# One layer of a hybrid encoder: two input products as one Winograd pair, weights of q and k kept split, the residual kept in the result's rows

## The chip, the core and the metric

The kernel runs on one core of a Trainium2 chip. The metric is the device time of one execution in microseconds; the median of several runs counts. TensorE (PE) multiplies, VectorE (DVE) and ScalarE (ACT) work on whole tiles of 128 partitions, GpSimd (POOL) computes powers and issues some DMAs, SyncE (SP) issues the other DMAs.

## The reference

One layer, 2048 rows of 1024 values, all in float32. The parts that matter here:

```
y = rmsnorm(h, pre_mix_g)                    # h = x, 2048 x 1024
z = y @ w_in                                 # 1024 x 2576
zu, zv, zq, zk, zvb, zg, zlr = split(z)      # 512, 512, 256, 256, 512, 512, 16 columns
a = gmlp_mixer(zu, zv, ...)                  # per 128 rows: layernorm(gelu(zv)), a product along the rows, times gelu(zu)
b = gla_mixer(zq, zk, zvb, zg, zlr, ...)     # gated linear attention, state carried over chunks of 64 rows, times silu(zg)
h = h + rmsnorm(concat(a, b) @ w_out, post_mix_g)
f = square(relu(rmsnorm(h, pre_ff_g) @ w_ff1)) @ w_ff2
out = h + rmsnorm(f, post_ff_g)
```

## The kernel before

**Products.** A float32 operand is held as two halves: hi, a copy rounded to the multiplier's format, and lo, the rest. `mm3` (L146 to L148) is one product of two such pairs and issues three matmuls: hi by lo, hi by hi, lo by hi. ScalarE makes hi with a cast, VectorE makes lo with a subtraction (`split_lo`, L143). `load_w` loads 128 rows of a weight into a tile of the ring `ws`, casts and splits it.

**First phase.** The 2048 rows go in four blocks b of 512 rows, each of four tiles of 128. `group` computes one set of columns of z for a block, in eight k-steps of four tiles by three matmuls; g, vb, v and u are 512 columns wide, q 272 (with zlr), k 256. Block 0 runs g, vb, q, k, v, u; the other blocks run vb, q, k, g, then `out_proj` of the block before (o, 16 steps), v, u. The four sums of each product lie in four PSUM banks and are evicted by `keep`: zq and zk by VectorE (L592), the rest by ScalarE with `lookup` (L301).

**Jobs.** After certain k-steps, `jobs.tick` runs pieces of the other work of a block, and so puts their matmuls between the groups' own: `gla` (decay products `cm` and `dc`, transposes `qk` of qe and ke, scores `sc`, updates `up`, the products `o`, transposes of zg), `spatial` (`mixd`), `gate` (zu times zv at L441, the sum of squares at L443, a power on POOL at L156, the scaling at L445, then transposes `pt` of zu by `put`, L286) and `hpost` (the rows of h after the mixer). A job is queued when its group is done and is stepped by the ticks that follow, so the gates of block b - 1 and the last chunks of its attention fall into the first steps of block b.

**Order.** In the first phase the order on TensorE is that of the code; on the other engines a scheduler orders the instructions. From the first FFN product on, the order of all engines is that of the code.

**FFN.** Both products are done in seven block products for eight (the table `WINO`: for p1 to p7 the left part, the right part and the bank chain A, B or C; s1 to s4 and t1 to t4 are sums of blocks). The first (banks `pf_`) keeps its result in `f_d`; the second (banks `po_`) runs in two passes over 1024 rows each, with eight chunks a pass, reads right-hand tiles `tt` from `t_d` and adds its banks into tiles `acc`.

**Result.** `hpost` stores the rows after the mixer to `h_d`. At the end of a pass `evac` puts for each half row of 128x512 a sum of squares, a root, a `scale` (L1092) and a `give` into a list, from which `some` takes units as the slots go by; `read_h` brings the rows of `h_d` back on POOL's queue, `give` adds them on VectorE (L512) and stores the sum to `out`, from POOL in pass 0 and from SP in pass 1.

## Time and profile before

| what | value |
|---|---|
| median of 3 runs | 2029.22 us (2028.96 to 2031.94) |
| the profiled execution | 2030.61 us, its span 2028.8 us |
| TensorE busy | 1991.7 us, 98% of the span |
| VectorE, ScalarE, POOL busy | 68%, 47%, 13% |
| mean granted clock of TensorE | 0.996 |
| DMA | 467.83 MB, 231 GB/s on average |
| last matmul | starts 13.65 us after 2000 us of the span |

The profile is one execution, recorded by the hardware. A busy time is the sum of an engine's instructions; a row of waits tells what an engine stood idle for before an instruction; the granted clock is the share of full speed that TensorE was given. The start of one instruction to the start of the next on TensorE is the pitch, since matmuls overlap.

### The profile page before, as it was taken

The numbers are of one execution on the slowest core, as the hardware profiler recorded it, in microseconds if no ns is written. First come the engines' busy times: TensorE is split into PE (matmuls) and PEld (weight loads), VectorE is DVE, ScalarE is ACT, GpSimd is POOL, SyncE is SP. The second block draws the span as 40 slices with busy tenths as digits, with TensorE's granted clock in tenths as the row PEclk, the third lists the DMA queues.
The fourth block names the chain that finished last, engine by engine and source line by source line (L and its number), as shares of the span: only waits on it lengthen the run. The fifth ranks groups of instructions, "written<-read, shape, count | busy, mean of one in ns | idle before, by whom it ended". The sixth has DMA issues, their size and how long they took to land.

```text
span 2028.8 us, 27534 instructions
## 1 busy us (share of the span) xinstructions
PE 1991.7 (98%) x9504; PEld 1650.7 (81%) x9504; DVE 1388.8 (68%) x2443; ACT 948.1 (47%) x1894; POOL 268.1 (13%) x442
## 2 busy tenths in 40 slices
PE   8999999999999999999999999999999999999996
PEld 7989888988888887888887888888888888788885
DVE  4484467236735756657678777665888888989877
ACT  5463465236433446566667766665212215222212
POOL 0020311002100200013331333320000002100011
PEclk9999999999999999999999999999999999999998
DMA  7434744535783586758888888888676778876674
GB/s 225 133 113 132 236 154 146 177 132 159 219 279 112 169 289 201 261 188 279 283 278 301 295 285 287 267 279 300 237 269 238 246 262 295 296 265 241 244 277 176
DMA packets 174683, 467.83 MB, mean 231 GB/s; under 512 B 24768, under 2 KB 49872, under 8 KB 160848
## 3 DMA queue, kind: packets, MB, share of 16 engines
q1 hardware_dynamic: 145376, 368.01, 53.7%
q0 software_dynamic: 29168, 98.06, 13.6%
q8 instruction: 75, 1.23, 0.2%
q14 instruction: 64, 0.52, 0.1%
HBM read 331.77 MB, written 134.22 MB: 230 GB/s over the span
## 4 chain that ended last, share of the span: by engine, by line
PE 55%; DVE 2%; DMA 2%; issue 1%; ACT 1%; POOL 0%; DVEq 0%; POOLq 0%; ACTq 0%; SPq 0%
PE pf_A L146 6%; PE pf_A L148 6%; PE pf_A L147 6%; PE po_A L147 5%; PE po_A L146 5%; PE po_A L148 5%; PE pf_C L146 3%; PE pf_C L148 3%; PE pf_C L147 3%; PE po_C L147 2%; PE po_C L146 2%; PE po_C L148 2%; PE pf_B L148 1%; PE pf_B L147 1%; PE pf_B L146 1%; PE po_B L147 1%
## 5 line engine op out<-in xcount | busy, mean ns | idle before, releaser
L512 DVE TENSOR_TENSOR acc<-acc,po_A 128x512 f32<-128x512 f32 x232 | 159.2, 687 | 47.9 <-PE po_A L148 33.6
L962 ACT CAST sh_s<-r 128x512 fp32r<-128x512 f32 x96 | 55.6, 618 | 170.2 <-PE po_A L148 93.5
L962 ACT CAST sh_a<-f 128x512 fp32r<-128x512 f32 x94 | 54.6, 618 | 127.9 <-DMA f<-f_d 94.9
L143 DVE TENSOR_TENSOR wl_s<-s,wh_s 128x512 fp32r<-128x512 f32 x96 | 66.2, 689 | 60.7 <-ACT wh_s L725 60.6
L146 PE MATMUL pf_A<-hl_t,wh_s 128*128 128x512 f32 x256 | 102.1, 399 | 5.1 <-ACT uy L907 2.5
L146 PE MATMUL pp_o<-wl_o,abh 128*128 128x512 f32 x256 | 102.9, 402 | 0.3 <-DVE h L469 0.2
L146 PE MATMUL po_A<-tt,sh_s 128*128 128x512 f32 x256 | 100.5, 393 | 2.7 <-DVE acc L512 2.6
L148 PE MATMUL pf_A<-hh_t,wl_s 128*128 128x512 f32 x256 | 101.6, 397 | 0.0
L146 PE MATMUL po_C<-tt,sh_s 128*128 128x512 f32 x256 | 100.4, 392 | 0.7 <-DMA tt<-t_d_b 0.7
L147 PE MATMUL pf_A<-hh_t,wh_s 128*128 128x512 f32 x256 | 100.9, 394 | 0.0
L147 PE MATMUL po_A<-tt,sh_s 128*128 128x512 f32 x256 | 100.8, 394 | 0.0
L147 PE MATMUL po_C<-tt,sh_s 128*128 128x512 f32 x256 | 100.8, 394 | 0.0
L148 PE MATMUL pp_o<-wh_o,abl 128*128 128x512 f32 x256 | 99.9, 390 | 0.0
L147 PE MATMUL pp_o<-wh_o,abh 128*128 128x512 f32 x256 | 99.7, 390 | 0.0
L148 PE MATMUL po_C<-tt,sl_s 128*128 128x512 f32 x256 | 99.5, 389 | 0.0
L148 PE MATMUL po_A<-tt,sl_s 128*128 128x512 f32 x256 | 99.5, 389 | 0.0
L146 PE MATMUL po_A<-tt,sh_a 128*128 128x512 f32 x248 | 97.6, 393 | 1.3 <-DMA tt<-t_d_t 1.1
L147 PE MATMUL po_A<-tt,sh_a 128*128 128x512 f32 x248 | 97.6, 394 | 0.0
L512 DVE TENSOR_TENSOR acc<-acc,po_C 128x512 f32<-128x512 f32 x120 | 82.4, 687 | 21.3 <-PE po_C L148 13.8
L148 PE MATMUL po_A<-tt,sl_a 128*128 128x512 f32 x248 | 96.4, 389 | 0.0
L143 DVE TENSOR_TENSOR wl_a<-w1s,wh_a 128x512 fp32r<-128x512 f32 x96 | 65.9, 688 | 42.4 <-ACT wh_a L725 42.2
L512 DVE TENSOR_TENSOR uy<-uy,pf_C 128x512 f32<-128x512 f32 x62 | 42.4, 684 | 42.1 <-ACT uy L909 40.4
(301 smaller groups left out, 5917.5 us busy)
## 6 DMA issues: line engine op xcount, KB each, us to landing
tt<-t_d_t SPq DMA_DIRECT2D x61, 1024.0 KB, 6.0
tt<-t_d_b SPq DMA_DIRECT2D x46, 1024.0 KB, 4.8
w1s<-in_w SPq DMA_DIRECT2D x64, 512.0 KB, 4.8
f<-f_d SPq DMA_DIRECT2D x64, 512.0 KB, 7.0
w2s<-in_w POOLq DMA_DIRECT2D x32, 512.0 KB, 6.5
t_d_t<-th_t POOLq DMA_DIRECT2D x64, 256.0 KB, 5.0
t_d_t<-tl_t POOLq DMA_DIRECT2D x64, 256.0 KB, 4.9
f_d<-ux SPq DMA_DIRECT2D x30, 512.0 KB, 5.8
```

Source lines behind the costliest of these rows:

```text
L143: v.tensor_tensor(out_lo, src, hi.bitcast(F32), ALU.subtract)
L146: pe.matmul(ps, ahi, blo, start=start, stop=False, **kw)
L147: pe.matmul(ps, ahi, bhi, start=False, stop=False, **kw)
L148: pe.matmul(ps, alo, bhi, start=False, stop=stop, **kw)
L512: eng.tensor_tensor(out_, x_, y_, ALU.add)
L962: a.copy(hi, src)
```

## The change

- `pair` computes vb and g of blocks 1 to 3 together, after k, as one product of a 512x1024 left side with a 1024x1024 right side in seven products of blocks: p1, p2, p5, p6, p7, p4, p3. Each takes four k-steps with two tiles of 128 rows. A chain (A, B or C) has two banks; p1, p6, p7 and p4 use chain A in turn, and its banks are copied out by ScalarE in between.
- `sums_w`, ticked in block 0, loads the rows of w_in for both groups, makes the four right-hand sums t1 to t4 and stores them to `v_d`.
- `load_s`, in every second k-step of group k, loads the rows of xt for two k again, scales them, makes the four left-hand sums and splits them.
- `load_q` stores the split weights of q and k to `q_d` in block 0 (32 stores from POOL) and loads the halves from there in the other blocks.
- The rows after the mixer are stored straight into `out`. `give` adds the scaled halves there by an accumulating DMA from POOL, except for rows 15, 10 and 11, which come back by SP and are added and stored as before.
- The sums of y for the FFN in block 3 (`sums(0, k)`) are queued after the pair and not before vb.

The core of the diff:

```diff
+    h_d = [out[i * P:(i + 1) * P, :] for i in range(NT)]
...
+    def load_q(b, g, k):
+        n = q_d[g, k].shape[-1]
+        if b == 0:
+            hi, lo = load_w(f"{b}_{g}", w_in, GROUPS[g], k)
+            pool.dma_start(q_d[g, k][:, 0, :], hi.bitcast(F32))
+            pool.dma_start(q_d[g, k][:, 1, :], lo.bitcast(F32))
+            return hi, lo
...
+        loads[f"{b}_{g}"] = dma.dma_start(hi.bitcast(F32), q_d[g, k][:, 0, :]).ins
+        dma.dma_start(lo.bitcast(F32), q_d[g, k][:, 1, :])
+        return hi, lo
...
+    def sums_w(k):
...
+            st = wp.tile([P, D], F32, name=f"vs{k}_{c}", tag="xr", bufs=4)
+            dma.dma_start(st, w_in[(k + 4 * c) * P:(k + 4 * c + 1) * P, 1536:2560])
...
+        minus(v, t1, b12, b11)
+        minus(v, t2, b22, t1)
+        minus(v, b12, b22, b12)
+        minus(v, b21, b21, t2)
+        for n, t in enumerate((t1, t2, b12, b21)):
+            dma.dma_start(v_d[k][:, n, :], t)
...
+    def load_s(b, k):
+        y1, y2 = stage(f"xs1_{b}_{k}"), stage(f"xs2_{b}_{k}")
+        for t, kk in ((y1, k), (y2, k + 4)):
+            dma.dma_start(t, xt[kk * P:(kk + 1) * P, b * TB:(b + 1) * TB])
+            a.activation(t, t, AF.Copy, scale=gpre[:, kk:kk + 1])
...
+        plus(v, a22, a21, a22)
+        minus(v, a21, a11, a21)
+        minus(v, a11, a22, a11)
+        minus(v, a12, a12, a11)
+        for n, t in enumerate((y1, y2)):
+            a.copy(hi[:, n * 512:(n + 1) * 512], t)
+            split_lo(lo[:, n * 512:(n + 1) * 512], t, hi[:, n * 512:(n + 1) * 512])
...
+    def pair(b, ss_):
...
+        for m, n in enumerate(PAIR):
...
+            for k in range(4):
+                if right[0] == "t":
+                    st = stage(f"ws_{b}_{n}_{k}")
+                    loads[f"{b}_pair"] = dma.dma_start(st, v_d[k][:, int(right[1]) - 1, :]).ins
...
+                    a.copy(wh, st)
+                    split_lo(wl, st, wh)
...
+                for t in range(2):
...
+                    mm3(chains[chain][t], *lh, wh, wl, k == 0 and not begun, k == 3, skip_group_check=True)
...
+                elif n == "p6":
+                    zg_[t] = slot(f"zg_{i0 + t}", tag="four")
+                    a.copy(zg_[t], A[t])
...
-            if b == NB - 1:
-                jobs.add(*((lambda k=k: sums(0, k), 1) for k in range(4)))
-            group(b, "vb", AF.Copy)
...
+            jobs.add(*((lambda k=k: sums_w(k), 1) for k in range(4)))
...
+        def before_k(k):
+            if b > 0 and k % 2:
+                ss_.append(load_s(b, k // 2))
...
-        group(b, "k", None)
+        group(b, "k", None, before_k)
         if b > 0:
-            group(b, "g", AF.Silu, lambda k: finish(b - 1, 1) if k == KT - 1 else None)
+            pair(b, ss_)
+        if b == NB - 1:
+            jobs.add(*((lambda k=k: sums(0, k), 1) for k in range(4)))
...
+    def give(i, hf):
+        cs = slice(hf * 512, (hf + 1) * 512)
+        if i in res:
+            plus(v, res[i][hf], res[i][hf], halves[i, hf])
+            dma.dma_start(out[i * P:(i + 1) * P, cs], res[i][hf])
+        else:
+            pool.dma_start(h_d[i][:, cs], halves[i, hf], accum_op=ALU.add)
...
+                    if final and slot_ % 28 == 4:
+                        for row_ in (2 * NPAIR - 1, NPAIR - 2, NPAIR - 1):
+                            read_h(p * 2 * NPAIR + row_)
```

TensorE at the start of block 2, before: behind the third k-step of vb stand the transposes `pt4_0` and `pt5_0` of the gated rows of tiles 4 and 5 of block 1. The number that ends a name tells tiles apart.

```order
L146 MATMUL pp_2_vb_3_3814<-wl_2_vb_2_3876,yh_2_2_3583 128x512
L147 MATMUL pp_2_vb_3_3814<-wh_2_vb_2_3875,yh_2_2_3583 128x512
L148 MATMUL pp_2_vb_3_3814<-wh_2_vb_2_3875,yl_2_2_3584 128x512
L286 MATMUL pt4_0_3891<-ident_213,zu_4_3779 128x128 x4
L286 MATMUL pt5_0_3900<-ident_213,zu_5_3781 128x128 x4
L146 MATMUL pp_2_vb_0_3811<-wl_2_vb_3_3912,yh_2_3_3626 128x512
L147 MATMUL pp_2_vb_0_3811<-wh_2_vb_3_3911,yh_2_3_3626 128x512
```

The same place after; `put` is at L402 and `mm3` at L151 to L153 there.

```order
L151 MATMUL pp_2_q_3_3984<-wl_q2_2_4042,yh_2_2_3755 128x272
L152 MATMUL pp_2_q_3_3984<-wh_q2_2_4041,yh_2_2_3755 128x272
L153 MATMUL pp_2_q_3_3984<-wh_q2_2_4041,yl_2_2_3756 128x272
L402 MATMUL pt4_0_4057<-ident_217,zu_4_3951 128x128 x4
L402 MATMUL pt5_0_4066<-ident_217,zu_5_3953 128x128 x4
L151 MATMUL pp_2_q_0_3981<-wl_q2_3_4076,yh_2_3_3798 128x272
L152 MATMUL pp_2_q_0_3981<-wh_q2_3_4075,yh_2_3_3798 128x272
```

The transposes still stand behind the third step of the block, which is now one of q, 272 columns wide. The decay products of chunks 2 and 3 in block 1 have moved from vb to q in the same way.

VectorE at that place, after: `xs1` and `xs2` are the left-hand sums of `load_s`, L557 and L561 are the gate's two steps (L441 and L445 before).

```order
L628 TENSOR_TENSOR xs2_2_0_4202<-xs1_2_0_4201,xs2_2_0_4202 128x256
L631 TENSOR_TENSOR xs1_2_0_4201<-xs1_2_0_4201 128x256
L557 TENSOR_TENSOR zu_4_3951<-zu_4_3951,zv_4_3600 128x512
L557 TENSOR_TENSOR zu_5_3953<-zu_5_3953,zv_5_3602 128x512
L631 TENSOR_TENSOR xs1_2_0_4201<-xs2_2_0_4202,xs1_2_0_4201 128x256
L160 TENSOR_SCALAR rs_a4_4000<-ssa4_3998 128x1
L631 TENSOR_TENSOR xs2_2_0_4202<-xs2_2_0_4202,xs1_2_0_4201 128x256
L549 TENSOR_TENSOR zv_6_3604<-mixd6_3965,bs_225 128x512
L561 TENSOR_SCALAR zu_4_3951<-zu_4_3951,rs_a4_4000 128x512
```

Sums of `load_s` now stand among the steps of the gate, where splits of vb's weights stood.

VectorE at the end of the kernel, before: `hr` is a residual's half row, L1092 the scale.

```order
L1092 SCALAR_TENSOR_TENSOR acc1_22_3_16598<-acc1_22_3_16598,rs_f15_18920,pfg_13916 128x512
L512 TENSOR_TENSOR hr15_1_18677<-hr15_1_18677,acc1_22_3_16598 128x512
L1092 SCALAR_TENSOR_TENSOR acc1_21_3_16701<-acc1_21_3_16701,rs_f15_18920,pfg_13916 128x512
L512 TENSOR_TENSOR hr15_0_18676<-hr15_0_18676,acc1_21_3_16701 128x512
L1092 SCALAR_TENSOR_TENSOR acc1_12_2_16542<-acc1_12_2_16542,rs_f10_18958,pfg_13916 128x512
```

After, from the last add of a product (`po15_B_3`) on:

```order
L628 TENSOR_TENSOR acc1_11_3_16843<-acc1_11_3_16843,po15_B_3_19225 128x512
L1202 TENSOR_TENSOR ssf10_19193<-ssf10_19193 128x1
L160 TENSOR_SCALAR rs_f10_19236<-ssf10_19193 128x1
L628 TENSOR_TENSOR hr15_18970<-hr15_18970,acc1_22_3_16928 128x512
L1202 TENSOR_TENSOR ssf11_19208<-ssf11_19208 128x1
L160 TENSOR_SCALAR rs_f11_19242<-ssf11_19208 128x1
L1208 SCALAR_TENSOR_TENSOR acc1_21_3_17015<-acc1_21_3_17015,rs_f15_19197,pfg_14248 128x512
L628 TENSOR_TENSOR hr15_18970<-hr15_18970,acc1_21_3_17015 128x512
```

Behind that add stood one residual's add and seven pairs of a scale and an add; one add and five pairs stand there now, since row 14's halves need no add on VectorE. All other rows of the result but 10 and 11 have lost that add too.

## Rows read from the trace of the kernel before

**Rows 1.** The page, busy time of each engine, share of the span, instructions.

```profile
PE 1991.7 (98%) x9504; PEld 1650.7 (81%) x9504; DVE 1388.8 (68%) x2443; ACT 948.1 (47%) x1894; POOL 268.1 (13%) x442
```

**Rows 2.** Waits of TensorE: who waits for whom, us in total, times, longest.

```profile
PE po_A L146 <- DVE acc L512: 2.6, 1, 2.6
PE pf_A L146 <- ACT uy L907: 2.5, 1, 2.5
PE pf_A L146 <- ACT u L907: 2.2, 1, 2.2
PE po_A L146 <- DMA tt<-t_d_t: 1.1, 1, 1.1
PE po_C L146 <- DMA tt<-t_d_b: 0.7, 1, 0.7
PE pf_A L146 <- ACT u L903: 0.4, 1, 0.4
```

**Rows 3.** Windows behind three waits: stretch, its length, busy by engine, PEclk, DMA share, GB/s.

```profile
779.44:782.86 3.42, 3.42 (x9) 2.53 (x9) 2.56 (x5) 3.10 (x6) 0.00 (x0) 0.50 0.49 153
1093.47:1096.88 3.41, 3.41 (x9) 2.65 (x8) 3.41 (x6) 3.41 (x8) 0.00 (x0) 0.50 0.40 162
1748.00:1752.00 4.00, 4.00 (x19) 3.30 (x18) 4.00 (x8) 0.00 (x0) 0.00 (x0) 1.00 1.00 312
```

**Rows 4.** Timeline of TensorE: start, duration, line, operation. FFN, then q's first, k's first.

```profile
1979.82 0.39 PE L146 MATMUL po_C<-tt,sh_s 128*128 128x512 f32 x1
1982.57 0.39 PE L146 MATMUL po_A<-tt,sh_s 128*128 128x512 f32 x1
...
52.29 0.28 PE L146 MATMUL pp_q<-wl_q,yh 128*128 128x272 f32 x1
64.32 0.28 PE L146 MATMUL pp_k<-wl_k,yh 128*128 128x256 f32 x1
```

**Rows 5.** Timeline of VectorE at the end of pass 1.

```profile
1991.49 0.74 DVE L1092 SCALAR_TENSOR_TENSOR acc<-acc,rs_f,pfg 128x512 f32<-128x512 f32 x1
...
2014.09 0.69 DVE L512 TENSOR_TENSOR acc<-acc,po_B 128x512 f32<-128x512 f32 x1
...
2015.89 0.74 DVE L1092 SCALAR_TENSOR_TENSOR acc<-acc,rs_f,pfg 128x512 f32<-128x512 f32 x1
...
2024.99 0.69 DVE L512 TENSOR_TENSOR hr<-hr,acc 128x512 f32<-128x512 f32 x1
```

**Rows 6.** DMA issues: count, KB each, median us from issue to landing.

```profile
out<-hr POOLq DMA_DIRECT2D x16, 256.0 KB, 8.2
```

**Rows 7.** Timeline of ScalarE in the first group: first and seventh cast of ws_g.

```profile
6.63 0.62 ACT L217 CAST wh_g<-ws_g 128x512 fp32r<-128x512 f32 x1 [0.45 <-DMA ws_g<-in_w_in]
...
19.10 0.62 ACT L217 CAST wh_g<-ws_g 128x512 fp32r<-128x512 f32 x1 [0.33 <-DMA ws_g<-in_w_in]
```

**Rows 8.** Groups by line, shapes apart: count, busy us, mean ns, idle before, releaser.

```profile
L143 DVE TENSOR_TENSOR wl_vb<-ws_vb,wh_vb 128x512 fp32r<-128x512 f32 x32 | 21.7, 688 | 16.2 <-ACT wh_vb L217 12.3 <-DMA trif<-in_sel 3.5
L592 DVE TENSOR_SCALAR zq<-pp_q,rx 128x272 f32<-128x272 f32 x16 | 6.9, 494 | 3.1 <-PE pp_q L148 3.1
L907 ACT COPY uy<-pf_A 128x512 f32<-128x512 f32 x31 | 18.1, 585 | 17.0 <-PE pf_A L148 15.5 <-DMA f_d<-ux 0.7 <-DMA f_d<-uy 0.7
```

**Rows 9.** Timelines of TensorE and VectorE, start of block 2; in brackets the idle before.

```profile
337.79 0.50 PE L146 MATMUL pp_vb<-wl_vb,yh 128*128 128x512 f32 x1 [0.75 <-ACT zu L301]
...
343.78 0.49 DVE L445 TENSOR_SCALAR zu<-zu,rs_a 128x512 f32<-128x512 f32 x1 [0.43 <-POOL rs_a L156]
...
346.41 1.03 PE L286 MATMUL pt<-ident,zu 128*128 128x128 f32 x8
...
347.55 0.49 DVE L445 TENSOR_SCALAR zu<-zu,rs_a 128x512 f32<-128x512 f32 x1 [0.44 <-POOL rs_a L156]
```

**Rows 10.** Timelines of VectorE and TensorE in vb of block 1.

```profile
143.43 0.42 DVE L143 TENSOR_TENSOR lal<-xs,lah 128x256 fp32r<-128x256 f32 x1
...
143.94 0.28 PE L333 MATMUL cm<-lal,trir 128*128 128x256 f32 x1
```

94 lines of the change are left out of this document (66 added, 28 removed).

## Prediction

> **What bounds the kernel now.** I read the page first. TensorE is busy for 1991.7 us, 98% of the span, VectorE for 68% [rows 1], so the time is its matmuls, its few waits, a start and a tail; no other engine comes near. Next I read its waits after the start; those that the argument needs are in [rows 2]: three of 2.2 to 2.6, which are the longest, and some of about 1 or less. Third, the granted clock: after two of these three waits TensorE ran 3.4 us at 0.50, its lower level of 1.2 GHz, and after the third it stayed at 1.00 [rows 3], so a wait of some 2 us may cost 1.7 us more. Fourth, the pitch of the matmuls: twelve of 128x512 start within 2.75 us, 0.229 each, and the 96 of a q group within 12.03 us, 0.125 each, so a k-step of twelve takes 2.75 us in a wide group and 1.50 in q [rows 4]. Everything beside this must be hidden behind these steps, and where a step is short, less is hidden.
>
> **What goes.** For each of blocks 1 to 3, vb and g were 2 x 8 x 12 = 192 matmuls and are 7 x 4 x 2 x 3 = 168. That is 3 x 24 = 72 fewer, at 0.229 **-16.5 us**, all on the bound engine. The Trainium skill ("TensorE: Matmul & The Clock Gate", Part 1) gives N/2.4 GHz + 2.5 ns, about 216 ns, for a back-to-back matmul; the pitch here is longer, and by the page's figure this term would be -15.5.
>
> At the end, rows of the result are accumulated by DMA in place of read, added and stored. VectorE ends 11.0 us after its last add of a product, which ended at 2014.09 + 0.60: one add of a residual, seven pairs of a scale and an add, 1.39 us a pair by their starts, and small ones [rows 5]. After, one add and five pairs stand there: 0.6 + 5 x 1.39 + 0.4 of small ones, 8.0. **-3.0** (-2 to -3.5: a root of the last two rows may come late). The reads of h go from 4 MB to 1.5 MB, so the last loads of tt should not wait: -1.1 and -0.7 [rows 2], **-1.8** (0 to -1.8, since SP now issues the three reads left ahead of two of those loads). In the middle, where pass 0 ends, VectorE loses sixteen adds of a residual and their waits for buffers, and the wait of 2.6 on acc [rows 2] should go: **-2.6**, or 0 if accumulating transfers hold the acc buffers for long. No row shows such a transfer; the nearest is out<-hr of the same size on the same queue, 8.2 us from issue to landing [rows 6], and I take that, at which the buffers come free some us before they are wanted. The Trainium skill ("DMA: Bandwidth & Descriptors", Anatomy of one DMA) fits 2.0 us + bytes/436e3 to a transfer issued from GpSimd, which makes 2.6 us of 256 KB as an estimate; no run here shows it, and the sum stays as it is by either. Together **-23.9**.
>
> **What comes, and what is moved.** The pair takes a right-hand tile of 256 KB for every six matmuls, 1.37 us, where a group took one per 2.75. In the first group ScalarE's casts of ws_g run from 6.63 to 19.10, seven of them, so six intervals, with a tile of xt in each: twelve tiles in 12.5 us, 1.04 each. A tile costs ScalarE a cast of 0.62 [rows 7] and VectorE a split of 0.69 [rows 8], both below 1.37, and no job is ticked into long waits there. So the pair itself costs nothing. The cost is in the cover that vb's and g's long steps gave to other chains:
>
> - **Gates of blocks 2 and 3.** The transposes of the gated rows stood after the third k-step of vb, 8.6 us into it. They now stand after the third of q, 4.5 us in, and the second two after the fourth. The chain's ends by the trace, counted from vb's start at 337.79: zu_5 at 343.78 + 0.49, 6.5 us; zu_7 at 347.55 + 0.49, 10.25 us [rows 9]. If it takes as long now, TensorE waits 6.5 - 4.5 = 2.0, spends 0.8 on transposes and 1.5 on a step, and waits 10.25 - 8.8 = 1.45: 3.4 a block, **+6.9**. In the chain two casts and three splits for vb and q go (q's weights arrive split), while the first two k of load_s bring four scalings and two casts to ScalarE and some eight subtractions of 128x256 and two splits to VectorE. That may move its end by 1.5 either way or, where a DMA of load_s is late, more: 0.5 to 6 a block.
> - **Block 1.** There the decay products cm stood behind the third k-step of vb, at 143.94, so vb began three steps, some 8.3, before; the operand of the second pair was written at 143.43 + 0.42, at +8.2, with nothing to spare [rows 10]. In q the first pair is wanted at +4.5 and the second 0.8 later: 8.2 - 5.3 = 2.9. The later steps (transposes of qe and ke, scores, the o products, transposes of zg) stand on q's and k's short steps too; by the same reckoning only the last comes late, by 0.6, and the yl and the sums of load_s ahead on VectorE may add 0.5. **+4.0** (1.5 to 6).
> - **The clock.** Each of these three places has a wait of 2 to 3 us. By [rows 3] two in three such waits lost 1.7 us; short matmuls around them may make it more or less likely. I take one and a half: **+2.5** (0 to 5.1).
> - **Block 0.** sums_w puts two loads of 512 KB and four subtractions per k into vb, q and k. A split of k's weights then stands behind four evictions of zq, 0.49 each, and three subtractions of 0.69 [rows 8]: 4.0 us, of which two steps hide most: **+1.5** (0 to 3). The loads stand on SP's queue ahead of some of xt and ws_g in the first group: **+0.4** (0 to 1). The stores of q's and k's halves are 32 issues on POOL's queue, which has nothing urgent there: nothing.
> - **Start of the pair.** VectorE evicts four zk, 2.0 us, behind or before the first splits: up to 1.3 a block, I take 0.3: **+1.0** (0 to 3.9).
> - **Banks.** p6, p7 and p4 share two banks. Between the last matmul of one tile and the next product's first stand three matmuls, 0.69 us, and ScalarE needs 0.585 for the copy of a bank [rows 8], after the matmul's end and perhaps behind a cast. The nearest row is a wait of 0.4 on such a copy [rows 2]. 0.2 at each of six places: **+1.2** (0 to 3).
> - **Block 3.** The four sums of FFN inputs are ticked later, into o, v and u, whose steps are long: **+0.3** (0 to 1).
>
> In all **+17.8**, so -6.1 net. The profiled execution took 2030.61 us, 1.8 more than its span, and would take 2024.5; the median of three runs was 2029.22, and from there it is **2023.1**, -0.3%.
>
> **The rivals.**
> A, the cover holds. For: 64 casts and splits of q's and k's weights are gone in blocks 1 to 3 from the two engines that feed the chains, and each of the chains has idle time in it, 0.43 and 0.44 us on VectorE before two of its scalings of zu [rows 9], which wait for POOL alone. Against: the positions in TensorE's order are earlier by 4 us and the chain needs some 6 to 10. Then about 4 of the 17.8 are left and the time is 2009.
> B, the losses eat the gain. Gates at 5 a block, block 1 at 5, three windows at half clock, the pair's start at 1 each: 10 + 5 + 5.1 + 3 + 1.5 = 24.6 against 23.9, so 2029 to 2030: no change.
> C, the pair isn't bound by TensorE, so the change does not do what it says: if tiles come at 1.60 us and not below 1.37, 84 of them cost 19 us, with the rest at its middle 2042. Against it stand [rows 7], at 1.04.
> D, slower by the accumulating transfers. They are 26, on one queue with eight in flight; if they run one after the other at the 8.2 us of [rows 6], the last pass has ten from the first scale at 1991.49 [rows 5] (some 16 earlier now), and the end moves from 2024 to about 2057. It decides from some 5.7 us each; below that the ten are done before the six stores that are left. For it: an accumulate reads what it writes. Against: reads of h of twice the size, four of them issued together, landed side by side.
>
> **How the numbers follow.** The forecast has 0.50, A 0.15, B 0.22, C 0.05, D 0.08. About 0.2% (4 us) is what a measurement of this kernel can tell from no change. The forecast's terms spread by some 7 us to either side (2016 to 2030), most from the gates. It gives 0.43 to faster and 0.07 to the same; A is faster; B is the same, with 0.04 of it slower; C and D are slower. So faster 0.58, the same 0.25, slower 0.17. The range runs from near A's time to past B's: 2011 to 2032, which leaves out D, C and the cheapest ends.
>
> **What would show it.** TensorE's instructions down by 72, its busy time by about 16 us. Waits of TensorE on zu or on the transposes' operand in the fourth k-step of q in blocks 2 and 3, 1 to 3 us each; one on lal in block 1; dips of the granted clock behind them. Inside the pair no waits but short ones on banks, a product of 24 matmuls in 5.5 us. No wait on acc near 1730, none on tt near the end, and five pairs of scale and add after TensorE's last matmul, 12 us or so to the end of the span in place of 15. It is wrong if a product of the pair takes over 6 us, if the accumulating transfers land after 10 us or in a row, or if q's steps show no wait at all (then A).

## The result: 1.5% slower, and where the time went

The changed kernel takes **2060.72 us** (median of 4 runs, 2058.15 to 2063.51) and the kernel before, beside it, 2029.09 (4 runs, 2027.84 to 2031.94): a ratio of **1.0153, interval 1.0141 to 1.0165**. That is slower by some 31 us where 6 less were forecast. The profiled execution has a span of 2061.4 us, 32.6 more than before.

The page of the profile after, its rows of busy time and of the granted clock (columns as in [rows 1]):

```profile
PE 1997.4 (97%) x9432; PEld 1649.2 (80%) x9432; DVE 1434.1 (70%) x2511; ACT 984.1 (48%) x1942; POOL 286.1 (14%) x464
...
PEclk9999999999999999999999999999999999999999
```

The 72 matmuls are gone, 9504 to 9432, yet TensorE is busy for 5.7 us more than in [rows 1], where 16 less were expected, and idle for 26.9 more (2061.4 - 1997.4 against 2028.8 - 1991.7). The first says that the same matmuls went slower somewhere, which is the clock or a spacing too small to be a wait; the second asks for the waits. The row of the clock can't tell, since a short stretch at half speed leaves a slice at 9.

Waits of TensorE after (columns as in [rows 2]), the longest groups:

```profile
PE pp_q L151 <- ACT zu L417: 8.9, 5, 3.1
PE pp_g L151 <- ACT yh L207: 6.9, 1, 6.9
PE pp_q L151 <- DVE wl_q L148: 5.6, 2, 4.2
PE pt L402 <- DVE zg L527: 4.4, 4, 2.3
PE po_C L151 <- DMA tt<-t_d_t: 3.3, 1, 3.3
PE pp_k L151 <- DVE wl_k L148: 3.1, 1, 3.1
PE pf_A L151 <- ACT uy L1028: 2.5, 1, 2.5
...
PE pp_o L151 <- DVE h L585: 2.1, 1, 2.1
PE pp_v L151 <- DVE zk L708: 1.9, 1, 1.9
...
PE pt L402 <- DVE zu L561: 1.2, 2, 0.7
```

Before, all waits came to 21.6 us, after to 51.4. The start (pp_g) was there, and the waits on uy and u as in [rows 2]. New are the first matmul of q on ScalarE's eviction of zu, 8.9 (before, vb's first waited 1.7 there, in two blocks together); q and k on their own weights, 8.7; transposes on zg; po_C on a load of tt; pp_o on h. The wait that the prediction was about, transposes on zu in q, is the last row: 1.2 in all.

Windows behind four of these waits (columns as in [rows 3]):

```profile
363.60:367.00 3.40, 3.24 (x13) 2.98 (x14) 3.38 (x9) 3.40 (x8) 0.71 (x1) 0.50 0.47 165
69.98:73.40 3.42, 3.42 (x18) 3.42 (x17) 2.27 (x6) 0.00 (x0) 2.51 (x5) 0.51 1.02 265
773.20:776.60 3.40, 3.40 (x10) 2.62 (x9) 3.05 (x5) 2.29 (x5) 0.00 (x0) 0.50 1.06 392
1746.00:1749.40 3.40, 3.40 (x10) 2.66 (x9) 0.00 (x0) 0.58 (x1) 0.86 (x1) 0.50 1.07 351
```

There are nine such stretches of 3.4 us at the lower level, 1.2 GHz, each behind a wait of 2.1 us or more, where before had the two of [rows 3]. Seven more by 1.7 us each are 12 us, more than half of what TensorE's busy time is above its forecast.

By stages, from the first matmul of each group in the timeline of TensorE (us, before and after, worked out from those starts):

| stage | before | after | difference |
|---|---|---|---|
| start, g and vb of block 0 | 52.3 | 52.9 | +0.7 |
| q and k of block 0 | 23.5 | 38.2 | **+14.7** |
| v and u of block 0 | 59.8 | 62.4 | +2.6 |
| block 1: vb, q, k, g; after: q, k, pair | 80.5 | 85.4 | **+4.8** |
| block 2, the same | 69.3 | 69.1 | -0.3 |
| block 3, the same | 69.4 | 69.0 | -0.4 |
| o, v, u of blocks 1, 2 and 3 | 361.4 | 369.1 | **+7.6** |
| the last o | 46.8 | 50.9 | **+4.1** |
| FFN, both products | 1250.4 | 1251.5 | +1.1 |
| last matmul to the end | 15.2 | 12.9 | **-2.3** |

They add up to 32.6. A wait ahead of q's first matmul stands in the row of the u before it, so 2.4 of each u's excess belongs to the next block's q.

The pair itself does what it should. In block 2 it runs from 393.46 to 432.81 without a wait:

```profile
393.46:432.81 39.35, 39.35 (x170) 31.29 (x169) 20.23 (x32) 21.42 (x34) 0.00 (x0) 1.00 0.64 202
```

168 matmuls in 39.35 us are 0.234 each, against the 0.229 of [rows 4], with the clock at 1.00, and VectorE and ScalarE are busy for little more than half of it. The groups that it replaces were shorter than [rows 4] say: g of blocks 2 and 3 took 21.8 us before, 0.227 a matmul. So a pair saves 2 x 21.8 - 39.4 = 4.2 us and not 24 x 0.229 = 5.5, some 12.6 in three blocks. The Trainium skill ("TensorE: Matmul & The Clock Gate", Part 1) gives about 216 ns for a back-to-back matmul of this width; all three pitches here are longer.

**First place: the start of q in blocks 1 to 3.** ScalarE and then TensorE at the start of block 2; L302 is the scaling in `load_s`, L417 the eviction of zu from PSUM:

```profile
356.37 0.72 ACT L302 ACTIVATE xs<-xs,gpre 128x512 f32<-128x512 f32 x1 [4.84 <-DMA xs<-in_xt]
362.41 0.72 ACT L302 ACTIVATE xs<-xs,gpre 128x512 f32<-128x512 f32 x1 [5.32 <-DMA xs<-in_xt]
363.04 1.82 ACT L417 ACTIVATE zu<-pp_u,rx 128x512 f32<-128x512 f32 x3
```

```profile
363.76 0.59 PE L151 MATMUL pp_q<-wl_q,yh 128*128 128x272 f32 x1 [2.60 <-ACT zu L417]
```

The scheduler put two scalings of `load_s` ahead of the evictions of zu. The second waits 5.32 us for its transfer, and behind it stand evictions that could have run: they free the PSUM banks that q needs. The last matmul of u starts at 358.98, before the wait for that transfer is over. TensorE waits 2.60 (2.40 and 3.09 in the other two blocks), and the clock is at half from 363.6.

**Second place: q and k of block 0.** SP's queue, then VectorE (L285 and L295 are the loads and stores of `sums_w`, L215 a load of weights, L631 its subtractions), then TensorE:

```profile
54.53 2.40 SPq L295 DMA_DIRECT2D v_d<-vt  x2
...
59.84 0.92 SPq L285 DMA_DIRECT2D vs<-in_w_in  x2
60.87 0.89 SPq L215 DMA_DIRECT2D ws_q<-in_w_in  x2
...
65.23 2.49 SPq L295 DMA_DIRECT2D v_d<-vt  x2
```

```profile
64.51 0.69 DVE L631 TENSOR_TENSOR vt<-vs 128x512 f32<-128x512 f32 x1 [2.86 <-DMA vs<-in_w_in]
66.67 0.69 DVE L631 TENSOR_TENSOR vt<-vs,vt 128x512 f32<-128x512 f32 x1 [1.47 <-DMA vs<-in_w_in]
...
69.00 0.44 DVE L148 TENSOR_TENSOR wl_q<-ws_q,wh_q 128x272 fp32r<-128x272 f32 x1 [0.44 <-ACT wh_q L222]
```

```profile
69.50 0.39 PE L151 MATMUL pp_q<-wl_q,yh 128*128 128x272 f32 x1 [4.22 <-DVE wl_q L148]
...
78.71 0.39 PE L151 MATMUL pp_k<-wl_k,yh 128*128 128x256 f32 x1 [3.06 <-DVE wl_k L148]
```

VectorE waits for vs with the splits of q's weights behind it; SP's stores wait for VectorE (8.2 us for vt from 52 to 92) with the loads of those weights behind them. A split of k's weights waits 5.1 us besides, for the store of an earlier half out of its buffer. The DMA engines are full there:

```profile
53.00:72.00 19.00, 13.44 (x98) 13.00 (x97) 9.03 (x17) 2.91 (x8) 6.22 (x13) 0.95 1.01 342
```

**Third place: the last o.** VectorE splits hl_b and hl_t for the FFN there, the sums that the change ticks later, and one waits 1.33 us for a cast, which itself waits 1.40 for its transfer; the eviction of pp_o stands behind, and TensorE waits 2.1 for it:

```profile
768.69 2.00 DVE L148 TENSOR_TENSOR hl_b<-hl_b,hh_b 128x512 fp32r<-128x512 f32 x3 [1.33 <-ACT hh_b L673]
770.67 0.69 DVE L148 TENSOR_TENSOR hl_t<-hl_t,hh_t 128x512 fp32r<-128x512 f32 x1
771.28 1.88 DVE L585 TENSOR_TENSOR h<-pp_o,pg 128x512 f32<-128x512 f32 x3
```

All three have one form: an instruction that waits for a transfer, itself or through a cast, stands on an in-order engine ahead of one that could run, and TensorE waits for the latter. The third is read from the trace alone: no run moves it, and the last o took 47.3 to 51.4 us in the other kernels that have the pair, which all tick these sums at the same place. The theory after this reading: the loss is the order in which the sums' instructions stand, not the bytes they move and not the products. Its rivals: the transfers themselves (DMA bandwidth), the stores of q's and k's halves, and the residual part.

### The profile page after: what moved, and what is told of

It reads as the page before. It is cut to its first block, busy times and chain, and to the rows that moved or that the text cites. A ratio compares the mean times of both kernels' runs of the same rounds, so it can differ in the third digit from the quotient of the medians.

```text
span 2061.4 us, 27763 instructions
## 1 busy us (share of the span) xinstructions
PE 1997.4 (97%) x9432; PEld 1649.2 (80%) x9432; DVE 1434.1 (70%) x2511; ACT 984.1 (48%) x1942; POOL 286.1 (14%) x464
## 4 chain that ended last, share of the span: by engine, by line
PE 58%; DVE 1%; ACT 1%; DMA 1%; issue 0%; DVEq 0%; ACTq 0%
PE po_A L152 6%; PE po_A L151 6%; PE pf_A L151 6%; PE po_A L153 6%; PE pf_A L153 5%; PE pf_A L152 5%; PE po_C L151 3%; PE po_C L152 3%; PE po_C L153 3%; PE pf_C L151 3%; PE pf_C L153 3%; PE pf_C L152 3%; PE po_B L152 1%; PE po_B L151 1%; PE po_B L153 1%; PE pf_B L151 1%
## 5 line engine op out<-in xcount | busy, mean ns | idle before, releaser
L628 DVE TENSOR_TENSOR acc<-acc,po_A 128x512 f32<-128x512 f32 x232 | 159.6, 688 | 60.6 <-PE po_A L153 32.1
L148 DVE TENSOR_TENSOR wl_s<-s,wh_s 128x512 fp32r<-128x512 f32 x96 | 66.2, 689 | 61.8 <-ACT wh_s L846 61.7
L151 PE MATMUL pf_A<-hl_t,wh_s 128*128 128x512 f32 x256 | 101.6, 397 | 5.1 <-ACT uy L1028 2.5
L151 PE MATMUL pp_o<-wl_o,abh 128*128 128x512 f32 x256 | 104.0, 406 | 2.2 <-DVE h L585 2.1
L151 PE MATMUL po_C<-tt,sh_s 128*128 128x512 f32 x256 | 101.7, 397 | 3.3 <-DMA tt<-t_d_t 3.3
L151 PE MATMUL po_A<-tt,sh_s 128*128 128x512 f32 x256 | 101.0, 394 | 0.0
L153 PE MATMUL po_C<-tt,sl_s 128*128 128x512 f32 x256 | 100.9, 394 | 0.0
L153 PE MATMUL pf_A<-hh_t,wl_s 128*128 128x512 f32 x256 | 100.9, 394 | 0.0
L153 PE MATMUL pp_o<-wh_o,abl 128*128 128x512 f32 x256 | 100.7, 393 | 0.0
L153 PE MATMUL po_A<-tt,sl_s 128*128 128x512 f32 x256 | 100.4, 392 | 0.0
L628 DVE TENSOR_TENSOR acc<-acc,po_C 128x512 f32<-128x512 f32 x120 | 82.5, 688 | 25.0 <-PE po_C L153 16.1
L151 PE MATMUL po_A<-tt,sh_a 128*128 128x512 f32 x248 | 97.8, 394 | 0.0
L153 PE MATMUL po_A<-tt,sl_a 128*128 128x512 f32 x248 | 97.3, 392 | 0.0
L161 POOL TENSOR_TENSOR rs_f<-rs_f,mhalf 128x1 f32<-128x1 f32 x16 | 13.5, 846 | 578.7 <-DVE rs_f L160 578.7
```

Source lines behind the costliest of these rows:

```text
L148: v.tensor_tensor(out_lo, src, hi.bitcast(F32), ALU.subtract)
L151: pe.matmul(ps, ahi, blo, start=start, stop=False, **kw)
L153: pe.matmul(ps, alo, bhi, start=False, stop=stop, **kw)
L161: pool.tensor_tensor(r, r, mhalf[:, :n], ALU.pow)
L628: eng.tensor_tensor(out_, x_, y_, ALU.add)
```

## The experiments

The shorter diffs stand against the changed kernel unless another is named. The kernel before, run beside these versions, took between 2028.24 and 2030.35 in its median. A time without an interval or a number of runs is that of one execution; the changed kernel's four spread by 5.4 us, so of such a time only a larger difference is read, and the stages come from its profile.

**The scalings of `load_s` behind the evictions of zu.** An explicit dependence in the scheduler holds `load_s` back until the last eviction of u has been issued.

```
+        behind = last["act"]          # the eviction of u issued last
...
-                ss_.append(load_s(b, k // 2))
+                with tc.issue_after(behind):
+                    ss_.append(load_s(b, k // 2))
```

> One edit to the changed kernel: ScalarE's instructions of load_s (scalings and casts) are queued behind the evictions of zu of the block before; before, two scalings stood ahead of them and waited up to 5 us for their DMA. If that place is the cause of the waits of q's first matmuls (2.4 + 0.55, 2.6, 3.1 us) and of the half clock behind them, u and q of the three blocks lose 2 us of waiting and about 1.5 of clock each: the whole falls by 8 to 11, to 2050 to 2053. The rival: load_s then comes too late, the pair waits for its left-hand sums, and the whole falls by less than 3.

2041.2 us, 17 to 22 less than the changed kernel's four runs and twice the gain that was expected. ScalarE at the start of block 2 now:

```profile
351.94 2.06 ACT L418 ACTIVATE zu<-pp_u,rx 128x512 f32<-128x512 f32 x3 [4.58 <-PE pp_u L153]
...
356.30 0.72 ACT L302 ACTIVATE xs<-xs,gpre 128x512 f32<-128x512 f32 x1
```

The three evictions start 4.4 us before the scaling, no group of waits on zu ahead of q is left, and the half-clock stretches at the starts of q are gone. The u of blocks 0, 1 and 2 took 30.5, 27.6 and 27.3 (33.0, 31.1, 30.9), q of blocks 1 to 3 25.7, 16.0 and 16.6 (27.2, 18.0, 18.0), k of block 1 15.4 (18.7). These seven stages give 17.9 of the 22.3 by which this profile's span is shorter. The FFN's second product was 4.7 shorter too, which this edit doesn't explain (it varied between 619 and 628 over all kernels), the last o 2.4, and vb to v of block 0 were longer by 3.5. The first place is shown: one ordering cost more than the 12.6 us that the pair brings.

**The sums of block 0 later, after k.**

```
-            jobs.add(*((lambda k=k: sums_w(k), 1) for k in range(4)))
...
         group(b, "k", None, before_k)
+        if b == 0:
+            jobs.add(*((lambda k=k: sums_w(k), 1) for k in range(4)))
```

> One edit to the changed kernel: the jobs sums_w are queued after group k of block 0 and so run beside v and u. In the changed kernel q and k of block 0 took 38.2 us against 23.5 before, and four waits and two stretches at half clock lie there. If sums_w is the cause, whether by its place on SP's queue or by the bytes it moves, q and k go back to 24 to 26 us and the whole to 2045 to 2049. If the stores of q's and k's split halves to q_d are the cause, q and k stay above 33 us and the whole above 2056. If sums_w only moves its price, v and u of block 0 (62.4 us together) grow by 5 or more.

2060.48, no change: q and k took 34.1, and u 52.1 in place of 33.0. The scheduler hoisted the first subtractions into q and k all the same, so they don't fall to 24 to 26. The growth of u has another cause than the text of the edit suggests: the jobs share one queue, and the four that now stand ahead of `gla` shift its steps. The decay products cm of the last two tiles, which stand behind the third step of block 1's q in the changed kernel, now run behind u's last step, with no step of a product between them to cover their chain:

```profile
153.53 0.58 PE L449 MATMUL cm<-lal,trir 128*128 128x256 f32 x1 [6.27 <-DVE lal L148]
...
161.63 0.58 PE L449 MATMUL cm<-lal,trir 128*128 128x256 f32 x1 [4.32 <-DVE lal L148]
```

TensorE waits 10.6 there in the two places and runs 17.1 us around it at half clock; no subtraction of `sums_w` is on VectorE at that time. As the products are gone from block 1, its q and k are 10.4 shorter (35.5 against 45.9), so the price of the move is less than u shows. This run therefore moves matmuls too and does not tell order from bytes.

**The sums' stores on POOL's queue.**

```
-            dma.dma_start(v_d[k][:, n, :], t)
+            pool.dma_start(v_d[k][:, n, :], t)
```

> One edit to the changed kernel: the four stores to v_d of each sums_w are issued from POOL and no longer from SP; the bytes moved are the same. If the loads of q's and k's weights were late because they stood on SP's queue behind stores that waited for VectorE, q and k of block 0 fall from 38.2 to 26 to 31 us, the whole to 2049 to 2055. If the DMA engines' time is the limit (busy 95% from 45 to 92 us), q and k stay within 2 us of 38.2 and the whole within 4 us of 2061.

2058.97. q and k 34.2 in place of 38.2, k alone 13.7 in place of 19.2 and q 20.5. The stores on SP are worth some 4 us of the 14.7 (vb ahead of q grew by 1.9, u fell by 1.6); with them away, q still waits. The total is within the spread of the changed kernel's runs.

**The residual part undone.** `read_h`, `give` and the root's bookkeeping as before, the pair kept.

```
-    h_d = [out[i * P:(i + 1) * P, :] for i in range(NT)]
+    h_d = [dram.tile([P, D], F32, name=f"h_d{i}") for i in range(NT)]
```

> The changed kernel with the residual part undone: rows go to a tensor of their own, are read back from POOL's queue, added on VectorE and stored, as in the kernel before. From the traces the tail lost 2.25 us by the change and the FFN products gained 1.05 (a wait of 3.3 on tt and a stretch at half clock came where a wait of 2.6 on acc and 1.8 on tt went). If both come from the residual part, the whole rises by 1 to 2, to 2062 to 2063. If the accumulating transfers (15.3 us from issue to landing) cost more than they save, it falls by 1 to 4.

2060.05: no difference. Its tail is 15.4 again, and it has none of the 3.3 on tt; its last o took 47.3. So the residual part neither caused nor paid for the 31 us.

**Without keeping q's and k's split weights.**

```
-                lambda k: load_q(b, g, k) if g in "qk" else load_w(f"{b}_{g}", w_in, GROUPS[g], k),
+                lambda k: load_w(f"{b}_{g}", w_in, GROUPS[g], k),
```

> The changed kernel with the keeping of q's and k's split weights undone: all four blocks load, cast and split them, nothing is stored to q_d. In the runs with sums_w moved or its stores on another queue q and k of block 0 still took 34 us against 23.5 before, and a split of k's weights waited 5.1 us on VectorE for a store of an earlier half (the six buffers of the ring are not free before their store has landed, 5 to 6 us). If the stores hold the ring, q and k of block 0 fall from 38.2 to 27 to 31 and the whole to 2050 to 2056, less what the casts cost in blocks 1 to 3. If sums_w alone fills block 0, q and k stay above 35 and the whole within 3 us of 2061.

2067.95, slower than each of the changed kernel's runs, by 4 to 10. In block 0 it gains (q and k 31.9), so the stores of the halves, that the prediction gave nothing, cost some 6 us there, and the u of blocks 0 to 2 are 2.5 to 3.2 shorter. In blocks 2 and 3 it loses more, 8 us each from q to the pair's end, since casts and splits of these weights are back among the sums: q and k of block 2 took 20.4 and 16.0, and the pair, 41.1, now waits:

```profile
PE pv_A L151 <- DVE wl_p L148: 6.1, 3, 2.9
```

**Keeping alone, in the kernel before.** `load_q` added to before, nothing else.

> The kernel before with one part of the change alone: q's and k's split weights are stored in block 0 and loaded in the others. If the stores hold the ring of weights, q and k of block 0 go from 23.5 to 29 to 34 us, with a stretch at half clock, and the whole to 2034 to 2041. If the part is free by itself, q and k stay below 25 and the whole is 2027 to 2031.

2027.45 beside 2028.24, with q and k of block 0 unchanged. The same 32 stores cost no time that can be seen where no sums stand beside them, so they are no cause of their own.

**Three edits at once**: `load_s` behind, no keeping, stores on POOL.

> The changed kernel with three edits together: load_s queued behind the evictions of zu on ScalarE, no keeping of q's and k's weights, the stores of v_d from POOL. From 2041 (the first edit alone) the other two should take the block 0's q and k from 40 to 25 to 29: 2027 to 2032. If the bytes of sums_w are what fills block 0, they stay above 33 and the whole above 2035. In blocks 2 and 3, q's eight steps, the transposes among them and the waits for the gates stay at 16 us against 12.0 for q alone: the wait that was predicted for the gates, 2 to 3 us a block, is not touched by these edits.

2057.11. q and k of block 0 are back at 24.8, but vb before them is 28.6 (21.8) with 6.8 us at half clock, and q and k of block 2 are 19.9 and 16.9. From vb to k it takes 53.4 in place of 60.0: 6.6 less, where the stores on POOL alone gave 2.1 and the lack of keeping 5.4, so the two gains nearly add up. What the lack of keeping loses in blocks 2 and 3 is more.

**Block 0's sums behind k's weights, with no keeping.** The sums' loads are issued after the last of k's, the jobs stand after k.

> As pair_lean, but the stores of v_d on SP and the loads of sums_w queued on SP behind the last weights of k, so that sums_w runs beside v and u of block 0 where a step is 2.75 us. q and k of block 0 should be at 23.5 to 25 us and v and u within 3 us of 60: 2022 to 2028. If sums_w carries its price with it, v and u grow by 6 to 15 and the whole is above 2030.

2069.45. q and k are whole, 23.5, so without the sums and the stores of the halves nothing there waits. u takes 49.8, again with 17.1 us at half clock: as in the run with the jobs after k, cm stands behind u's last step and waits 9.5. So this u, too, is the shifted order of the jobs and not a measure of the sums.

**The sums written into v's steps.** A sum's loads before an even step of v, its subtractions before the odd one, `load_s` behind the evictions.

```
+            with tc.issue_after(loads["0_k"]):
+                dma.dma_start(st, w_in[(k + 4 * c) * P:(k + 4 * c + 1) * P, 1536:2560])
...
+        def before_v(k):
+            if k % 2 == 0:
+                made.append(sums_w(k // 2))
+                next(made[-1])
+            else:
+                next(made[-1], None)
```

> The changed kernel with load_s queued behind the evictions of zu (2041 alone) and with sums_w written out in the steps of v in block 0, its loads behind the last of k's weights on SP. In the runs so far sums_w cost 11 to 15 us beside q and k (11 MB in 23.5 us) and 19 beside u (14 MB in 30 us); v has 2 MB of its own in 29 us, and with the 8 MB of sums_w 340 GB/s. If bytes in too short a time are the price, q and k are at 23.5 to 25, v at 29 to 33, u at 30.5, and the whole at 2023 to 2028. If the waits of SP's queue for VectorE are the price, v grows by 8 or more and the whole is above 2032.

2040.36, ratio 1.0048 (1.0032 to 1.0065). q is at its 12.0 again, k 16.8, v 31.9 and u 36.3. No job is queued for the sums here, and no cm stands behind u's last step.

**The same, with the sums' stores on POOL.**

> As v_fit, with the stores of v_d issued from POOL. If only bytes count, the same as v_fit within 2 us. If the order on SP's queue counts, v is shorter than in v_fit by 3 or more. Both fall together to 2023 to 2028 if the first theory holds.

2036.81 (4 runs), 1.0033 (1.0017 to 1.0048): the best version with the pair, and still slower than before. Against the stores on SP u is 5.5 shorter (30.8), and not v, as the expectation had it if the order on that queue counts. k takes 18.1. VectorE and TensorE at its end (L634 subtractions, L711 evictions of k):

```profile
76.38 0.69 DVE L634 TENSOR_TENSOR vt<-vs 128x512 f32<-128x512 f32 x1 [3.85 <-DMA v_d<-vt]
...
78.97 0.69 DVE L634 TENSOR_TENSOR vt<-vs,vt 128x512 f32<-128x512 f32 x1 [0.30 <-DMA v_d<-vt]
80.23 0.69 DVE L148 TENSOR_TENSOR wl_v<-ws_v,wh_v 128x512 fp32r<-128x512 f32 x1 [0.57 <-ACT wh_v L222]
...
82.24 1.65 DVE L711 TENSOR_SCALAR zk<-pp_k,rx 128x256 f32<-128x256 f32 x4
```

```profile
82.77 0.79 PE L151 MATMUL pp_v<-wl_v,yh 128*128 128x512 f32 x1 [6.42 <-DVE zk L711]
```

The first subtraction waits 3.85 for a buffer whose store hasn't landed, and k's evictions, which free the banks of v, stand behind all of them. It is the first place's form once more, on VectorE.

**Subtractions behind k's evictions.** Against the one before: `with tc.issue_after(last["k"])` around each sum's second half.

> As v_fit_pool (2036.8), with the subtractions of sums_w queued on VectorE behind the evictions of zk of block 0; bytes, places and queues of the loads and stores stay. If the order on VectorE is the cause of the 6.4 us before v and of the half clock there, k goes from 18.1 to 11.5 to 13 us and the whole to 2027 to 2031. If the bytes are the cause, v or u take what k gives, by 5 or more, and the whole stays above 2033.

2039.11, 1.0044 (1.0028 to 1.0061). k falls to 14.8 and v rises from 32.7 to 41.2: TensorE's scores wait there for qtm, 4.6 at the longest. That growth is what the expectation gave for bytes as the cause. By the trace ScalarE's copies into qtm stand behind a cast of u's weights that waits 3.63 for its load, and on VectorE steps of the decay chain stand behind subtractions that wait 3.60 for a load and 1.89 for a store. Late transfers and their place in the queues act together here, and this run doesn't separate them.

**`load_s`'s subtractions behind q's evictions too.**

```
-                with tc.issue_after(behind):
+                with tc.issue_after(behind), tc.issue_after(last["q"]):
```

> As zk_first, with the subtractions of load_s queued on VectorE behind the evictions of zq as well. If their place ahead of zq and of the gates' steps is the cause, the waits of k on zq (1.2, 1.8) go, q of blocks 2 and 3 falls from 16.4 to 14 to 15.5, and the whole lies 4 to 8 below zk_first, at 2021 to 2026, under both kernels. If the left-hand sums then come late, the pair grows from 39.4 by 2 or more a block and the whole is above zk_first.

2052.09, 1.0114 (1.0095 to 1.0134). q of blocks 2 and 3 drops to 14.3 and 14.5, and the pair's weights are late in turn (the wait for the first stands in k, 16.4 and 16.7):

```profile
PE pv_A L151 <- DVE wl_p L148: 9.8, 2, 5.1
...
PE sc L490 <- DVE qtm L485: 5.3, 3, 3.8
```

**Subtractions on GpSimd.** Against the version with the stores on POOL: `minus(pool, ...)`, and block 0's product kd from GpSimd to VectorE.

> As v_fit_pool (2036.8), with the sixteen subtractions of sums_w done by GpSimd in place of VectorE, and the products kd of block 0 on VectorE in their place, so that nothing which TensorE needs soon stands behind a subtraction that waits for its load. The same bytes move beside v. If the order on VectorE was the price, k of block 0 goes from 18.1 to 11.5 to 13 us, v stays below 32.7, and the whole is 2026 to 2031. If the bytes are, k or v stay as long and the whole stays above 2033.

The profiled execution took 2041.2 (another took 11338, which the trace of the first can't explain, so the time gives no verdict). VectorE and GpSimd beside each other:

```profile
73.75 7.78 DVE L148 TENSOR_TENSOR wl_v<-ws_v,wh_v 128x512 fp32r<-128x512 f32 x3 [1.19 <-ACT wh_v L222]
```

```profile
73.86 1.30 POOL L634 TENSOR_TENSOR vt<-vs,vt 128x512 f32<-128x512 f32 x1
75.12 1.29 POOL L634 TENSOR_TENSOR vs<-vs,vs 128x512 f32<-128x512 f32 x1
76.36 1.27 POOL L634 TENSOR_TENSOR vs<-vs,vt 128x512 f32<-128x512 f32 x1
```

Three splits that take 0.69 each elsewhere are busy for 7.78 us while GpSimd subtracts. Moving the work to the idle engine blocks VectorE instead. The Trainium skill ("SBUF — State Buffer", Who interferes with whom) says that a VectorE instruction with two SBUF inputs contends with a GpSimd instruction that reads SBUF; the trace agrees, at these numbers.

**One load at a time.** Each of the sums' loads behind one of v's weights, subtractions behind k's evictions.

> As v_fit_pool (2036.8), with each 512 KB load of sums_w queued on SP behind another load of v's weights, so that no more than about 0.75 MB stands ahead of a weight, and the subtractions, on VectorE again, one k-step later and behind the evictions of zk. If the burst of loads was the price, q and k of block 0 are 23.5 to 25 us, v below 32, u 30.5, and the whole is 2025 to 2030. If the 8 MB cost the same wherever they lie, q, k, v and u of block 0 stay 10 us or more above the 83.3 of the kernel before, and the whole above 2034.

2040.58, 1.0053 (1.003 to 1.0076). k 14.2, v 42.3, scores waiting up to 6.6 on qtm. Pacing the transfers in this way doesn't help: the copies into qtm again stand behind a cast of u's weights, which waits 4.50 for its load.

**The bytes alone, first try.** The kernel before with 8 MB of loads that nothing reads, issued on POOL's queue beside q and k of block 0.

> The kernel before with nothing but eight pairs of loads of 512 KB, as large as those of sums_w, added from POOL beside q and k of block 0: 8 MB that nobody reads, no work on VectorE, nothing on SP's queue. Loads and stores of sums_w move as many bytes. If bytes are the price, q and k go from 23.5 to 28 to 36 us, with a stretch at half clock, and the whole to 2034 to 2044. If queues and VectorE are the price, q and k stay below 25 and the whole within 3 us of 2029.

2039.72, but it is not the test that was meant: the queue had nothing ahead, the loads ran at once, and the first 30 us bore them (DMA share 0.94; the first group took 30.5 in place of 24.3). q and k stayed at 23.5. Inconclusive on its question.

**The bytes alone, second try.** The same 8 MB on SP, two loads of 512 KB at every second step of q and k, behind the weights loaded by then; no instruction waits for them.

```
+                    with tc.issue_after(loads[list(loads)[-1]]):
+                        dma.dma_start(st, w_in[(k // 2 + 4 * c) * P:(k // 2 + 4 * c + 1) * P, 1536:2560])
```

> The kernel before with sixteen loads of 512 KB added on SP, each pair between the weights of two steps of q or k of block 0; nobody reads them. 8 MB more in 23.5 us, with 2 MB of the kernel's own there and the next ones. If bytes alone are the price of sums_w, q and k go from 23.5 to 31 to 38 us with a stretch or two at half clock, as in the changed kernel (38.2), and the whole to 2037 to 2046. If the waiting of VectorE and ScalarE for them is the price, q and k stay below 27 and the whole below 2034.

2031.33 (8 runs), 1.0012 (0.9994 to 1.0031): no measurable difference. Windows of q and k of block 0:

```profile
52.40:64.50 12.10, 12.10 (x97) 12.02 (x96) 2.28 (x6) 3.67 (x8) 0.00 (x0) 1.00 1.01 344
64.50:76.00 11.50, 10.40 (x86) 10.19 (x86) 5.46 (x13) 3.93 (x9) 0.00 (x0) 1.00 0.97 341
```

The DMA engines are as full as in the changed kernel, 344 GB/s against 342, and q and k take 24.9, with one wait of 1.1 on wl_k. So full DMA engines are some 1.4 us of the 14.7 (by loads alone, where the sums have half loads and half stores). Beside q and k the bandwidth falls as the main cause; what the two kernels don't share is the instructions that wait for these transfers in front of others, and the stores. No run tests the bytes alone beside v and u, where the later versions put the sums.

**The residual part alone, in the kernel before.**

> The kernel before with the residual part alone: rows stored in the result and scaled halves accumulated there by DMA for 13 of 16 rows. The tail should lose 2.5 us (12.9 against 15.15 and 15.42 from the last matmul to the end in the runs with and without the part). The wait of 2.6 on acc should go; but the accumulating transfers took 11.8 to 15.3 us from issue to landing in place of 8.2, and the second FFN product took from 620.9 to 628.1 us in the kernels with them, 619.8 to 623.0 without. So 2025 to 2029; at 2031 or more the transfers cost the FFN more than the tail gains.

2027.16 (10 runs) beside 2029.55, 0.9986 (0.9976 to 0.9996). Its tail is 12.3 us, 2.9 less than before.

**Keeping and residual, no pair.**

> The kernel before with two of the change's parts, the keeping of q's and k's split weights and the residual in the result's rows, without the pair. Alone the first gave 2027.45 beside 2028.2 (one run) and the second 0.9986 (0.9976 to 0.9996). If they add up and the pair with its sums is all of the loss: 2024 to 2028, ratio 0.997 to 0.999, and the changed kernel lies 33 to 36 us above it. If they disturb each other: 2029 or more.

**2026.66** (10 runs) beside 2030.35, **0.9981 (0.997 to 0.9992)**: faster than both kernels, by no more than the residual part alone can give. Its page:

```profile
PE 1990.5 (98%) x9504; PEld 1651.4 (82%) x9504; DVE 1354.8 (67%) x2369; ACT 928.1 (46%) x1846; POOL 288.4 (14%) x464
```

It does 72 matmuls more than the changed kernel and has TensorE busy for 7 us less. The changed kernel is 34 us above it, and what the two don't share is the pair with its sums, and the FFN's sums queued later.

## Why the prediction was wrong

**What held.** The count and the pair: 72 fewer matmuls, 39.35 us a pair without waits, 1.41 a tile, so rival C (tiles at 1.60 us, 2042) is out by mechanism. The gain of the matmuls was 12.6 and not 16.5, since the pitch was taken from the FFN (0.229) for the groups that go (0.227) and for the pair (0.234). The tail: five pairs of a scale and an add, the last ending 8.1 us after the last add of a product, as worked out, and 2.3 to 2.9 us saved for the 3.0 of the sum. VectorE from the last add of a product to its end (L628 adds):

```profile
2048.94 0.69 DVE L628 TENSOR_TENSOR acc<-acc,po_B 128x512 f32<-128x512 f32 x1
...
2057.07 0.69 DVE L628 TENSOR_TENSOR hr<-hr,acc 128x512 f32<-128x512 f32 x1
```

The waits on tt near the end, 1.8, are gone too. The banks (1.2) and the pair's start (1.0) cost no wait. The first group (0.4) took as long as before; the 0.7 in the table lies ahead of its first matmul, which started between 5.9 and 7.9 us over all kernels.

**The step that failed: "Gates of blocks 2 and 3".** It counted `load_s`'s four scalings and two casts in those chains and said that a late DMA might make them later, 0.5 to 6 a block. But it had no place for those scalings ahead of the gate: they stand before the evictions of zu, one block boundary earlier, so TensorE lost 2.4 to 3.1 before q began and 1.7 by the clock behind it, in each of three blocks. The experiment that moves them gives 17.9 us on the stages that it touches. [rows 9] show a wait of 0.75 on zu ahead of vb; the step read its neighbours and passed over this one, the sign that the boundary had little slack. The order of ScalarE at the end of u would have shown the two scalings there.

The chain that the step worked out did end where it said, but TensorE was late too. VectorE's second scaling of zu in block 2, then the transposes:

```profile
369.40 0.49 DVE L561 TENSOR_SCALAR zu<-zu,rs_a 128x512 f32<-128x512 f32 x1 [0.44 <-POOL rs_a L161]
```

```profile
370.00 1.03 PE L402 MATMUL pt<-ident,zu 128*128 128x128 f32 x8
...
374.15 0.63 PE L402 MATMUL pt<-ident,zu 128*128 128x128 f32 x4 [0.69 <-DVE zu L561]
```

zu_5 is ready 6.1 us after q's start (6.5 in the forecast), and q's third step, slowed by the half clock, ends at 6.2 and not 4.5; so the waits were 0.3 and 0.7. With the scalings moved q runs at full clock, and the chain is faster: zu_5 after 3.9 us and zu_7 after 7.8, for 6.5 and 10.25. There the waits on zu are 0.4 in block 2 and 1.2 in block 3, and k waits 1.4 and 1.2 for the evictions of zq. Blocks 2 and 3 then take 2.2 and 1.7 us less than before from their start to o; with 4.2 saved by each pair, 2.0 and 2.5 were lost, for the 3.45 a block of the step. So it was too high for what it named and had the dear place at nothing. Why the chain is faster is not shown; rival A gave the casts and splits that go as a reason (it counts 64, by the traces they are 48 casts and 48 splits in blocks 1 to 3).

**"Block 0" was mis-sized: 1.5, measured 14.7** (3.4 of it two half-clock stretches). The step priced the engines' own time, evictions and subtractions, 4.0 us with two steps hiding most. It did not price a wait for vs in front of a split, nor SP's stores in front of the weights' loads, nor "The stores of q's and k's halves ... nothing", which were some 6 beside the sums and nothing without them. It counted SP's queue as a price in the first group alone. Of the 14.7, the runs give some 4 to SP's stores, some 6 to the stores of the halves and 1.4 to full DMA engines, each from a run of its own. They may overlap, and the rest is not shared out.

**"Block 1": 4.0.** From its first matmul to o the changed block took 4.8 longer; with the 4.2 that its pair saves, 9.0 were lost, 3.4 of it by the clock. With the scalings behind zu the block takes 80.4, as before, so 4.1 are lost there, 1.7 of them by the clock: about the forecast's size once the first place is gone. I made no experiment on its inner chain alone.

**"The clock": 2.5, measured 12.** One and a half more stretches were expected and seven came. Behind each of the eight waits of 2.1 to 4.2 us that came new the granted clock fell. Two in three such waits lost it in [rows 3], and the forecast took that rate; here it was nine of ten, and there were more of them.

**"Block 3": 0.3, and the last o took 4.1 more.** The FFN's sums were moved "into o, v and u, whose steps are long", but a long step doesn't help an eviction that stands behind a late split.

**The accumulates.** The wait of 2.6 on acc went, as forecast, and in its place po_C waits for tt:

```profile
1745.20 0.47 PE L151 MATMUL po_C<-tt,sh_s 128*128 128x512 f32 x1 [3.27 <-DMA tt<-t_d_t]
```

with 1.7 at half clock behind it. The profiles of all the kernels with the residual part have this wait, 3.2 to 3.3 us, and those of before and of the kernel without it don't, though the loads of tt are issued at the same place. What makes these loads late is not shown. The value taken from [rows 6], 8.2 us, was the wrong row: the transfers took 11.8 in the median of all and 15.3 in the middle of the FFN, past the 10 us that the prediction set as a sign of being wrong. DMA issues from 1715 to 1790 after (columns as in [rows 6]):

```profile
out<-acc POOLq DMA_DIRECT2D x16, 256.0 KB, 15.3
```

They also land in a row: the sixteen of pass 0 landed one after another from 1732.4 to 1772.0, 2.6 us apart in the mean. Yet rival D is out, since that is less than the 5.7 from which it would decide: six were issued within 5.4 us and overlap, the ten of the last pass landed 3.6 to 7.2 us after issue, and the tail is short.

**Sum.** Losses of 17.8 were expected and gains of 23.9. The gains came but for 3.9 of the matmuls and for acc; the losses were some 49 (32.6 on the span, and 12.6, 2.3 and 1.8 of gains that came). Rival B had the right kind of cause (the losses eat the gain) at half its size, and the time lies outside the range by 29 us. Of the 32.6 on the span, waits of TensorE account for +30, the clock for +12, the tail for -2.3 and the matmuls for -12.6. That leaves some 6 us in spacings that are no waits in the profile. I have not placed them.

**What stays open.** Block 0's sums were given seven other places, and vb to u of that block took 115 to 137 us in all of them, against 105.1 before and 122.4 in the changed kernel. In two of the seven the jobs' order moved matmuls out of block 1's q into that u as well. I did not find a place that is free, and have not shown that there is none. Moving the FFN's sums back before the last q was not tried. Beside the kernel with the two other parts, the best version with the pair takes 10.3 us more in block 0, 2.7 less in block 2 (q to u) and 2.0 more in block 3, where the FFN's sums are; as they are ordered here, three blocks don't pay for the sums that are made once.

## What to carry to other kernels

Price a new chain of loads not by its engine time but by what stands behind its first waiting instruction on each in-order engine and queue: a scaling of 0.72 us that waits 5.3 for its transfer cost more, placed ahead of an eviction, than the product it served could save (17.9 us against 12.6). Read the changed order at the boundaries between groups, where evictions free the banks of the next group, before reading it inside them, and count a half-clock stretch as part of a wait's price: here 1.7 us behind nine of ten waits of 2.1 to 4.2. Take the pitch of a product from the product itself. Before reading a moved job as a test of the engine that it loads, check that TensorE's own order stayed. When a change has several parts, time each alone: here two small parts were a gain of 0.2% and the large one took it back some nine times over.
